# The first norm's sums as products, four modulation blocks as products, and rotary angles computed first

## The chip, the cores and the metric

The kernel is one program on one core of a Trainium2 chip. The metric is device time in microseconds (us). The kernel before takes 1474.31 us, the median of three runs (1472.94 to 1475.11).

## The reference, cut to what matters

A trunk of two layers with 512 tokens and 1024 features, in float32. Only the start of layer 0 matters here.

```python
cond = silu(c)                                    # c: (1, 1024)
mod = cond @ ada_w[l] + ada_b[l]                  # 6144 values: shift, scale, gate, twice
h = rms_norm(x, norm_mix[l]) * (1 + scale) + shift
proj = h @ w_in_even                              # MLA columns and RWKV-7 columns
y_a = mla_mix(proj[..., :MLA_COLS], positions)    # rotary angles: positions * inv_freq
y_b = rwkv7_mix(proj[..., MLA_COLS:])             # 8 heads of 64, a scan over tokens
```

Layer 0 sends the two mixers' outputs through one output projection, then comes a feed-forward block; layer 1 is another linear recurrence and a second feed-forward block.

## The kernel before, in words

The activations lie transposed: features on the 128 partitions, tokens along the free dimension, so `xT[0..7]` are eight tiles of 128x512. Each weight tile is split into a high part (the float32r cast of `split`, ScalarE, L192) and the remainder (VectorE, L193), and `mm3` (L212 to L214) multiplies high by high, low by high and high by low. I call each of these 128x512 products a **main product**.

The engines are TensorE (PE; PEld is its weight load), VectorE (DVE), ScalarE (ACT), GpSimd (POOL) and SyncE (SP), which issues all loads here. Each engine runs its own instructions in program order; the scheduler that builds the program sets this order by priorities and estimated times, so an instruction of a later part can stand between those of an earlier one.

The start runs so:

- `cond` is one row. ScalarE takes its Silu (L287), then two PE products with a row of ones (L431) spread it over 128 partitions, and two copies (L432) bring it back to SBUF.
- The first norm: ScalarE squares each `xT[k]` (`Stats.add`, L268), VectorE adds the eight squares up (L266, L259), PE sums them over partitions by four 128x1 products (L275), `rsqrt` is ten small VectorE operations (L228 to L243), and `token_bc` spreads the result by four products (L283).
- Modulation: `ada(l, j)` loads one 128x1024 block of `ada_w` in two halves, multiplies each by `cond` on VectorE with a running sum (L301), and ScalarE adds the bias (L308) and makes the gain (L312).
- Then for each k, `mod_tile` makes the high and low parts of h (L317, L320, L321), a weight tile is loaded and split, and 18 main products follow: 144 in all. The first one needs L320 of k = 0.

After that come the four head pairs p = 0 to 3 of RWKV. `rw_prep` is a chain over all engines: sums of squares (L510), `rsqrt`, a transpose (L250), a scan, `k2` (L533), a product (L540), and the scaled operands (L551 to L560). `a_mats` then makes the 32 small blocks by products (L573), which VectorE and ScalarE copy out (L576, L581). Main products of later projections fill PE between these. After pair 3 a triangular system is solved on VectorE (L617 to L647), and PE goes on with its result at L658. Projections and scores of MLA lie beside it.

The rotary angles (L808 to L825) are computed with features on partitions, in seventeen VectorE steps over 128x512 elements (a cast, a multiplication, and three range reductions with L815, L816 and L818 among them), then one Sin on ScalarE goes into `trig`.

## Time and profile before

| | |
|---|---|
| median of three runs | 1474.31 us |
| profiled execution, its own time | 1476.02 us |
| span of its profile (first to last instruction) | 1473.7 us |
| busy: PE, DVE, ACT, POOL | 1414.1, 851.9, 574.7, 21.7 us |
| granted TensorE clock, mean | 0.975 |

The span and the 2.3 us around it make the profiled execution's time. PE is busy for 96% of the span, so what matters is where PE has nothing to do and where it runs below its full clock. In the page's 40 slices of 36.8 us that is the first slice, where PE is busy for half the time, and slices 4 to 7 (110 to 258 us), where it is busy for seven to nine tenths and its granted clock is lower in places.

### The profile page before, as it was taken

What the parts mean: (1) busy time and instruction counts of PE and PEld (TensorE: products, weight loads), DVE (VectorE), ACT (ScalarE), POOL (GpSimd) and SP (SyncE); (2) the same over time, 40 slices, a digit from 0 to 9 for tenths busy, and PEclk for the clock granted to TensorE, in tenths of its full rate; (3) what the DMA queues carried; (4) which work ended last, traced back from release to release, by engine and by line L of the source; (5) the groups of instructions that cost most, each with busy time, mean ns of one, the idle gap of its engine ahead of it and who ended that gap; (6) DMA issues with size and microseconds to landing.
All of it is one profiled execution on the core that took longest, in us unless ns stands there. A gap on an engine that the chain in (4) does not pass through costs nothing.

```text
span 1473.7 us, 21313 instructions
## 1 busy us (share of the span) xinstructions
PE 1414.1 (96%) x8526; PEld 1126.2 (76%) x8526; DVE 851.9 (58%) x1683; ACT 574.7 (39%) x1018; POOL 21.7 (1%) x38
## 2 busy tenths in 40 slices
PE   5999978989999999999999999999999999999996
PEld 4776748867778878888888777777788888888885
DVE  6887795687787765333347566566574333333343
ACT  4665536455554342222235444444343222222220
POOL 2000000000000000000000000000000000000000
PEclk9998897989999999999999999999999999999998
DMA  8630221063548875322232221211123223322221
GB/s 279 212 102 36 72 101 59 9 215 115 190 151 276 266 241 182 118 97 92 70 109 74 101 73 59 73 69 62 54 77 129 86 70 99 118 99 97 64 84 58
DMA packets 57061, 167.06 MB, mean 113 GB/s; under 512 B 6337, under 2 KB 6913, under 8 KB 56962
## 3 DMA queue, kind: packets, MB, share of 16 engines
q1 hardware_dynamic: 56962, 165.70, 33.7%
q8 instruction: 67, 1.10, 0.3%
q14 instruction: 32, 0.26, 0.1%
HBM read 163.58 MB, written 2.10 MB: 112 GB/s over the span
## 4 chain that ended last, share of the span: by engine, by line
PE 85%; DVE 9%; ACT 2%; DMA 2%; issue 1%; SPq 0%; POOL 0%; DVEq 0%; ACTq 0%; POOLq 0%
PE t L212 24%; PE t L214 24%; PE t L213 23%; DVE t L301 2%; DMA t<-in_ada 1%; PE t L573 1%; DVE t L193 1%; PE t L250 1%; PE t L928 1%; PE t L908 1%; PE t L1063 1%; PE t L1076 1%; PE t L721 1%; PE t L727 1%; PE t L275 1%
## 5 line engine op out<-in xcount | busy, mean ns | idle before, releaser
L212 PE MATMUL t<-t,t 128*128 128x512 f32 x1632 | 652.6, 400 | 6.4 <-ACT t L320 4.8
L213 PE MATMUL t<-t,t 128*128 128x512 f32 x1632 | 650.9, 399 | 1.6 <-DVE t L193 1.5
L214 PE MATMUL t<-t,t 128*128 128x512 f32 x1632 | 648.1, 398 | 1.4 <-DVE t L193 1.3
L193 DVE TENSOR_TENSOR t<-t,t 128x1024 fp32r<-128x1024 f32 (+3 forms) x287 | 286.5, 1013 | 254.0 <-ACT t L192 251.4
L192 ACT CAST t<-t 128x1024 fp32r<-128x1024 f32 (+3 forms) x287 | 247.9, 879 | 341.0 <-PE t L214 175.0
L212 PEld LDWEIGHTS t<-t,t 128*128 128x128 f32 x1632 | 308.8, 189 | 76.5 <-ACT t L320 5.9
L213 PEld LDWEIGHTS t<-t,t 128*128 128x128 f32 x1632 | 308.5, 189 | 72.7 <-DVE t L193 4.2
L214 PEld LDWEIGHTS t<-t,t 128*128 128x128 f32 x1632 | 308.4, 189 | 71.1 <-DVE t L193 1.9
L301 DVE SCALAR_TENSOR_TENSOR t<-t,cond 128x512 f32<-128x512 f32 (+1 forms) x128 | 119.8, 952 | 20.9 <-DMA t<-in_ada 20.5
L390 DVE TENSOR_TENSOR t<-t,t 128x512 f32<-128x512 f32 x44 | 30.4, 690 | 89.6 <-PE t L214 89.6
L389 ACT ACTIVATE t<-t 128x512 f32<-128x512 f32 x42 | 25.0, 595 | 127.0 <-PE t L214 127.0
L330 DVE SCALAR_TENSOR_TENSOR t<-t,mod,t 128x512 f32<-128x512 f32 x40 | 29.8, 750 | 56.1 <-PE t L214 56.1
L306 ACT ACTIVATE mod<-t,c_prm 128x1 f32<-128x1 f32 x64 | 18.7, 295 | 93.6 <-DVE t L301 93.5
L908 PE MATMUL t<-t,t 128*128 128x128 f32 (+3 forms) x64 | 26.1, 514 | 8.1 <-DVE t L904 6.0
L268 ACT ACTIVATE t<-t 128x512 f32<-128x512 f32 x40 | 25.0, 629 | 18.3 <-DVE t L330 14.0
L320 ACT ACTIVATE t<-t,mod 128x512 fp32r<-128x512 f32 x32 | 22.4, 720 | 22.3 <-DVE t L317 22.3
L928 PEld LDWEIGHTS t<-t,t 128*128 128x128 f32 x160 | 23.3, 205 | 9.9 <-ACT t L926 7.2
L1083 DVE TENSOR_TENSOR t<-t,t 128x256 f32<-128x256 f32 x56 | 23.5, 419 | 10.4 <-PE t L1076 10.4
L250 PE MATMUL t<-cst,t 128*128 128x128 f32 x148 | 24.0, 287 | 3.4 <-DVE t L878 1.4
L928 PE MATMUL t<-t,t 128*128 128x64 f32 x160 | 25.5, 291 | 0.7 <-ACT t L926 0.7
L1063 PEld LDWEIGHTS t<-t,t 128*32 128x32 f32 x1280 | 13.9, 112 | 14.6 <-issue 9.9
L317 DVE SCALAR_TENSOR_TENSOR t<-t,gA,t 128x512 f32<-128x512 f32 x32 | 23.2, 741 | 2.9 <-PE t L283 2.9
(251 smaller groups left out, 1120.6 us busy)
## 6 DMA issues: line engine op xcount, KB each, us to landing
t<-in_ada SPq DMA_DIRECT2D x64, 512.0 KB, 4.3
t<-in_fu SPq DMA_DIRECT2D x44, 512.0 KB, 3.3
t<-in_fg SPq DMA_DIRECT2D x44, 512.0 KB, 3.3
t<-in_win SPq DMA_DIRECT2D x40, 512.0 KB, 3.2
t<-in_ada SPq DMA_DIRECT2D x64, 256.0 KB, 4.7
t<-in_fd SPq DMA_DIRECT2D x32, 384.0 KB, 3.1
t<-in_fd SPq DMA_DIRECT2D x32, 320.0 KB, 2.9
t<-in_xT SPq DMA_DIRECT2D x16, 256.0 KB, 3.9
```

The source lines that it names most:

```text
L192: S_.copy(hi[:, :n], raw[:, :n])
L193: V.tensor_tensor(out=lo[:, :n], in0=raw[:, :n], in1=hi[:, :n].bitcast(F32), op=ALU.subtract)
L212: TE.matmul(ps, a, xh, start=first and q == 0, stop=False)
L213: TE.matmul(ps, b, xh, start=False, stop=False)
L214: TE.matmul(ps, a, xl, start=False, stop=last and q == n - 1)
L250: TE.transpose(ps[:, blk(b)], src[:, blk(b)], ident)
L301: V.scalar_tensor_tensor(out=w, in0=w, scalar=1.0, in1=cond[:, n:n + m], op0=ALU.mult, op1=ALU.mult, accum_out=a[:, q:q + 1])
L330: V.scalar_tensor_tensor(out=xT[k], in0=ps, scalar=gate, in1=xT[k], op0=ALU.mult, op1=ALU.add)
L390: V.tensor_tensor(out=sg, in0=dense(PA, I[f"fu{l}"][j], hs), in1=sg, op=ALU.mult)
L908: TE.matmul(sps[:, :nk], mla["q"][:, blk(i)], kT[par][:, :nk], start=True, stop=True)
L928: TE.matmul(ops[:, i * 64:(i + 1) * 64], pT[:, blk(j)], vn[j][:, h * 64:(h + 1) * 64], start=j == 0, stop=j == i)
L1063: TE.matmul(lps[w:w + 32, c * 16:c * 16 + 16], kk[:, sl], half(q[:, sl], 1), start=True, stop=True, tile_position=(0, w))
```

## The change

1. `ada_pe` computes the modulation blocks j = 8, 0, 9, 1 (scale and shift of k = 0 and 1) on PE: the block is loaded with input features on partitions and multiplied by `condT`, `c` as eight columns, in eight 128x1 products each. Blocks 8 and 0 stand ahead of k = 0, 9 and 1 ahead of k = 1. The four blocks are loaded into `A_all`, whose memset moves behind the projection.
2. The squares of the first norm are no longer added by VectorE: each goes to PE at once, four 128x1 products for each k, 32 in all.
3. The angles are computed at the start, with tokens on partitions: 64 values on a partition, then 256. Sin stays where it was, on a broadcast view; four PE transposes and a copy make `trig`.
4. ScalarE issues four small loads (`cT`, the identity, positions, frequencies); `prm` is loaded between `xT[3]` and `xT[4]`.
5. `k2` of `rw_prep` is done by ScalarE. The sums of squares of the MLA latents take four products for each of five tiles (20) in the place of eight products and three VectorE adds.

```diff
     cond = cp.tile([P, D], F32, name="cond")
     nc.sync.dma_start(out=cond[0:1], in_=I["c"])
+    condT = cp.tile([P, KT], F32, name="condT")
+    nc.scalar.dma_start(out=condT, in_=I["cT"])
+    cst = cp.tile([P, CST.n], F32, name="cst")
+    nc.scalar.dma_start(out=cst[:, :P], in_=I["cst"][:, :P])
     xT = [X_() for _ in range(KT)]
-    for k in range(KT):
-        nc.sync.dma_start(out=xT[k], in_=I["xT"][k])
-    prm = load(cp, "prm", PRM.n)
...
     S_.activation(cond[0:1], cond[0:1], AF.Silu)
+    S_.activation(condT, condT, AF.Silu)
...
+    def ada_pe(l, j, ap, w, ps):
+
+        nc.sync.dma_start(out=w, in_=ap)
+        for k in range(KT):
+            TE.matmul(ps, w[:, blk(k)], condT[:, k:k + 1], start=k == 0, stop=k == KT - 1)
+        scales(l, j, ps, bias=pr("ada_b", 48 * l + j))
...
+        pos, freq = trig[:, :NB].bitcast(I32), w[:, 2 * n:2 * n + 16]
+        nc.scalar.dma_start(out=pos, in_=I["pos"])
+        nc.scalar.dma_start(out=freq, in_=I["freq"])
+        for k in range(KT):
+            nc.sync.dma_start(out=xT[k], in_=I["xT"][k])
+            if k == 3:
+                nc.sync.dma_start(out=prm, in_=I["prm"])
...
+            reduce(TWO_PI * 4096.0, [c * 4096.0 for c in (PI2_A, PI2_B, PI2_C)])
+            reduce(TWO_PI, (PI2_A, PI2_B, PI2_C))
...
-            G.memset(A_all, 0.0)
...
-                stats = Stats(D, M_)
+                ss, cols = PP(), PP()
                 for k in range(KT):
-                    stats.add(xT[k])
-                stats.close()
-                rb = token_bc(stats.end(PP), PP)
+                    sq = M_()
+                    S_.activation(sq, xT[k], AF.Square)
+                    for b in range(NB):
+                        TE.matmul(ss[:, b:b + 1], sq[:, blk(b)], ones, start=k == 0 and b == 0,
+                                  stop=k == KT - 1 and b == NB - 1)
+                first = lambda j, i: ada_pe(0, j, I["ada0p"][i], A_all[:, 1024 * i:1024 * i + 1024], cols[:, i:i + 1])
+                first(8, 0)
+                w = wload(I["win0a"][0], 768)
+                first(0, 1)
+                rb = token_bc(rsqrt(ss[:, :NB], NB, 1.0 / D, EPS), PP)
                 ps6 = [PA() for _ in range(6)]
                 for k in range(KT):
-                    ada(0, 8 + k, RP)
-                    ada(0, k, RP)
+                    if k == 1:
+                        first(9, 2)
+                        first(1, 3)
+                    elif k:
+                        ada(0, 8 + k, RP)
+                        ada(0, k, RP)
                     hs.append(mod_tile(0, 0, k, rb, M_, HR))
...
+            G.memset(A_all, 0.0)
...
-                V.tensor_scalar(out=k2, in0=a, scalar1=pr("k_a", p), scalar2=oka[:, p:p + 1],
-                                op0=ALU.mult, op1=ALU.add)
+                S_.activation(k2, a, AF.Identity, scale=pr("k_a", p), bias=oka[:, p:p + 1])
...
-        V.tensor_scalar(out=ang, in0=ang, scalar1=cs_("invf"), scalar2=None, op0=ALU.mult)
...
-        S_.activation(trig, ang, AF.Sin)
+        sin = X_()
+        S_.activation(sin.rearrange("p (b w s) -> p b w s", b=NB, w=2),
+                      trig[:, :256].rearrange("p (b s) -> p b s", b=NB).unsqueeze(2).to_broadcast([P, NB, 2, 64]), AF.Sin)
+        ps = PO()
+        transpose4(ps, sin)
+        S_.copy(trig, ps)
...
-            if j in (0, 2):
-                acc = sq
-            else:
-                V.tensor_tensor(out=acc, in0=acc, in1=sq, op=ALU.add)
...
+            for b in range(NB):
+                TE.matmul(sums[:, 4 * q + b:4 * q + b + 1], sq[:, blk(b)], means[:, q:q + 1],
+                          start=j == 0 and b == 0, stop=j == 4 and b == NB - 1)
```

The order of instructions moves in three places that matter below. The first is PE's start. Before, from its first row on (L431 spreads `cond`, L275 sums the squares, L283 spreads the norm, L212 is the first main product):

```order
L431 MATMUL t_133<-cond,trig 128x512
L431 MATMUL t_136<-cond,trig 128x512
L275 MATMUL t_187<-ones,t_164 128x1 x4
L283 MATMUL t_207<-cst,t_205 128x128 x4
L212 MATMUL t_212<-t_237,t_243 128x512
```

After, from the products of the eighth square on (L510; 28 like them stand ahead, behind the two that spread `cond`; L310 are the blocks 8 and 0, L279 is `token_bc`, L208 the first main product):

```order
L510 MATMUL t_190<-ones,t_234 128x1 x4
L310 MATMUL t_191<-condT,t_167 128x1 x8
L279 MATMUL t_282<-cst,t_280 128x128 x4
L310 MATMUL t_191<-condT,t_167 128x1 x8
L208 MATMUL t_287<-t_295,t_253 128x512
L209 MATMUL t_287<-t_295,t_254 128x512
```

Behind the two products that spread `cond`, 52 products now stand ahead of the first main product, where 8 stood. After the first 18 main products come 16 more of L310 (blocks 9 and 1).

The second place is PE at pair 2, behind L540 (L592 now), whose result VectorE needs for nothing that L573 (L625 now) reads. Before:

```order
L214 MATMUL t_2370<-t_567,t_2366 128x512
L212 MATMUL t_2407<-t_237,t_2403 128x512
L540 MATMUL t_1180<-t_906,cst 128x512
L573 MATMUL t_1199<-t_1184,t_1186 128x128 x2
L573 MATMUL t_1207<-t_1184,t_1186 128x128
L573 MATMUL t_1199<-t_1185,t_1187 128x128 x2
L573 MATMUL t_1207<-t_1184,t_1186 128x128
```

After, where 18 main products stand between L592 and the first L625; these are the last four of them and what follows:

```order
L208 MATMUL t_2414<-t_622,t_2410 128x512
L209 MATMUL t_2414<-t_622,t_2411 128x512
L210 MATMUL t_2414<-t_623,t_2410 128x512
L208 MATMUL t_2455<-t_295,t_2451 128x512
L625 MATMUL t_1256<-t_1241,t_1243 128x128 x2
L625 MATMUL t_1264<-t_1241,t_1243 128x128
L625 MATMUL t_1256<-t_1242,t_1244 128x128 x2
```

The pair's products L573 came right behind L540; now a row of main products lies between. Up to the first L573 of pair 3, PE has 420 main products in both orders.

The third place is VectorE at pair 2, just ahead of these products (L557 and L559 make what L573 reads, L818 is a step of the angles). Before:

```order
L541 TENSOR_TENSOR bv_125<-t_1180,t_1047 128x512
L553 TENSOR_TENSOR t_1185<-t_1129,t_1138 128x2x2
L560 TENSOR_TENSOR t_1186<-t_1058,t_1131 128x2x2x64
L557 SCALAR_TENSOR_TENSOR t_1129<-t_1129,t_1056 128x512
L818 SCALAR_TENSOR_TENSOR t_2343<-t_2342,t_2343 128x512
L559 TENSOR_TENSOR t_1186<-t_1129,t_1131 128x2x128
L559 TENSOR_TENSOR t_1187<-t_1129,t_1131 128x2x128
L560 TENSOR_TENSOR t_1187<-t_1058,t_1131 128x2x2x64
L818 SCALAR_TENSOR_TENSOR t_2343<-t_2342,t_2343 128x512
L456 SCALAR_TENSOR_TENSOR t_1262<-t_1237,c_prm,t_1262 128x511
```

After, the same rows of the pair (L609 and L611 are L557 and L559):

```order
L612 TENSOR_TENSOR t_1243<-t_1115,t_1188 128x2x2x64
L609 SCALAR_TENSOR_TENSOR t_1186<-t_1186,t_1113 128x512
L611 TENSOR_TENSOR t_1243<-t_1186,t_1188 128x2x128
L611 TENSOR_TENSOR t_1244<-t_1186,t_1188 128x2x128
L612 TENSOR_TENSOR t_1244<-t_1115,t_1188 128x2x2x64
L497 SCALAR_TENSOR_TENSOR t_1319<-t_1294,prm,t_1319 128x511
L628 COPY_PREDICATED t_167<-msk,t_1256 128x4x128
```

The steps of the angles are gone from between the pair's operations. Elsewhere on VectorE, in the solve from L617 to the last L647, the weight splits L193 fall from four to three, the adds L843 from two to none, the modulation steps L301 from four to two and the steps L904 from two to one; the adds are removed, and the others stand ahead of the solve or behind it.

## Rows read from the trace of the kernel before

**Rows 1.** Page, parts 1 and 4: busy time by engine; the chain that ended last.
```profile
PE 1414.1 (96%) x8526; PEld 1126.2 (76%) x8526; DVE 851.9 (58%) x1683; ACT 574.7 (39%) x1018; POOL 21.7 (1%) x38
...
PE 85%; DVE 9%; ACT 2%; DMA 2%; issue 1%; SPq 0%; POOL 0%; DVEq 0%; ACTq 0%; POOLq 0%
```

**Rows 2.** Timeline of the first 40 us: start, us, engine, line, operation, idle before it.
```profile
0.73 1.28 ACT L287 ACT_TABLE_LOAD   x1 [0.73 <-PEq L1208]
...
1.15 3.67 SPq L163 DMA_DIRECT2D t<-in_xT  x8
...
2.28 1.05 ACT L287 ACTIVATE cond<-cond 1x1024 f32<-1x1024 f32 x1 [0.27 <-DMA cond<-in_c]
...
3.38 3.78 PE L431 MATMUL t<-cond,trig 1*128 1x512 f32 x4 [3.38 <-ACT cond L287]
...
9.98 1.15 ACT L268 ACTIVATE t<-t 128x512 f32<-128x512 f32 x2
...
13.51 1.86 PE L275 MATMUL t<-ones,t 128*128 128x1 f32 x8 [6.34 <-DVE t L259]
...
15.41 0.16 DVE L228 TENSOR_SCALAR t<-t 128x4 f32<-128x4 f32 x1 [1.35 <-PE t L275]
...
19.38 0.15 DVE L243 TENSOR_TENSOR t<-t,t 128x4 f32<-128x4 f32 x1
...
19.59 2.07 PE L283 MATMUL t<-cst,t 128*128 128x128 f32 x8 [4.22 <-DVE t L243]
...
21.41 0.30 ACT L308 ACTIVATE t<-t,half_b 128x2 f32<-128x2 f32 x1 [0.41 <-DVE t L301]
...
22.49 0.72 ACT L320 ACTIVATE t<-t,mod 128x512 fp32r<-128x512 f32 x1
...
23.26 0.80 PE L212 MATMUL t<-t,t 128*128 128x512 f32 x1 [1.59 <-ACT t L320]
...
24.28 0.63 PE L212 MATMUL t<-t,t 128*128 128x512 f32 x1
...
24.71 0.63 PE L213 MATMUL t<-t,t 128*128 128x512 f32 x1
```

**Rows 3.** Windows: stretch, us, busy time of PE, PEld, DVE, ACT, POOL, granted clock, DMA.
```profile
40.00:50.00 10.00, 10.00 (x44) 8.00 (x44) 10.00 (x26) 5.83 (x17) 0.00 (x0) 1.00 0.95 323
...
135.47:155.00 19.53, 19.17 (x65) 15.54 (x66) 11.98 (x28) 8.83 (x15) 0.00 (x0) 0.50 0.16 54
...
175.00:222.00 47.00, 36.29 (x155) 25.54 (x155) 44.64 (x93) 17.97 (x36) 0.00 (x0) 0.93 0.26 90
...
420.50:423.40 2.90, 0.00 (x1) 0.00 (x0) 2.19 (x4) 1.52 (x4) 0.00 (x0) 1.00 0.79 305
...
424.66:428.08 3.42, 3.42 (x8) 2.75 (x9) 3.42 (x6) 2.41 (x5) 0.00 (x0) 0.50 0.00 0
```

**Rows 4.** Timeline of PE near 788 us: four 128x1 products between main products.
```profile
787.93 0.95 PE L275 MATMUL t<-ones,t 128*128 128x1 f32 x8
...
788.74 0.48 PE L212 MATMUL t<-t,t 128*128 128x512 f32 x1
```

**Rows 5.** Timeline of PE, 110 to 140 us: pair products before and in the slow stretch.
```profile
111.40 2.05 PE L573 MATMUL t<-t,t 64*128 64x128 f32 x16
...
135.47 3.78 PE L573 MATMUL t<-t,t 64*128 64x128 f32 x16 [2.84 <-DVE t L559]
```

**Rows 6.** The chain that ended last, 0 to 245 us: start, us, engine, line.
```profile
118.37 1.07 PE t L510 x8
...
150.71 1.50 PE t L510 x8
```

**Rows 7.** Groups of DVE by line, 175 to 220 us: xcount, busy, mean ns, idle before.
```profile
L193 DVE TENSOR_TENSOR t<-t,t 128x1024 fp32r<-128x1024 f32 x4 | 4.9, 1216 | 0.1
...
L301 DVE SCALAR_TENSOR_TENSOR t<-t,cond 128x1024 f32<-128x1024 f32 x4 | 4.8, 1212 | 0.0
...
L843 DVE TENSOR_TENSOR t<-t,t 128x512 f32<-128x512 f32 x2 | 1.4, 682 | 0.0
```

More of the change, by code (lines that the diff above doesn't have):

```diff
@@ L71 @@
 CST = Cols()
-for _n, _k in (("ident", 128), ("cent", 128), ("BB", 128), ("B2", 2), ("invf", 1), ("phase", 1)):
+for _n, _k in (("ident", 128), ("cent", 128), ("BB", 128), ("B2", 2)):
     CST.add(_n, _k)
@@ L95, in _const_arrays @@
     put(c, CST, "B2", np.stack([i < 64, i >= 64], 1))
-    f = np.concatenate([INV_FREQ, INV_FREQ, -INV_FREQ, INV_FREQ])
-    put(c, CST, "invf", np.concatenate([f, f])[:, None])
-    ph = np.concatenate([np.full(32, np.pi / 2), np.zeros(32)])
-    put(c, CST, "phase", np.concatenate([ph, ph])[:, None])
     s, t = i[:, None] % 64, i[None] % 64
@@ L160, in _body @@
     nc.sync.dma_start(out=cond[0:1], in_=I["c"])
+    condT = cp.tile([P, KT], F32, name="condT")
+    nc.scalar.dma_start(out=condT, in_=I["cT"])
+    cst = cp.tile([P, CST.n], F32, name="cst")
+    nc.scalar.dma_start(out=cst[:, :P], in_=I["cst"][:, :P])
     xT = [X_() for _ in range(KT)]
-    for k in range(KT):
-        nc.sync.dma_start(out=xT[k], in_=I["xT"][k])
-    prm = load(cp, "prm", PRM.n)
-    cst = cp.tile([P, CST.n], F32, name="cst")
-    nc.sync.dma_start(out=cst[:, :P], in_=I["cst"][:, :P])
+    prm = cp.tile([P, PRM.n], F32, name="prm")
     ones, means = cp.tile([P, 1], F32, name="ones"), cp.tile([P, 2], F32, name="means")
@@ L303, in ada, with scales @@
             n, q = n + m, q + 1
-        mod, i = mods[l][:, j:j + 1], 48 * l + j
+        i = 48 * l + j
         if q == 1:
-            S_.activation(mod, a[:, 0:1], AF.Identity, bias=pr("ada_b", i))
+            scales(l, j, a[:, 0:1], bias=pr("ada_b", i))
         else:
-            S_.activation(a, a, AF.Identity, bias=half_b[:, i:i + 1], accum_out=mod)
+            scales(l, j, a, bias=half_b[:, i:i + 1], accum_out=mods[l][:, j:j + 1])
+    def ada_pe(l, j, ap, w, ps):
[3 more added lines that the diff above has]
+        scales(l, j, ps, bias=pr("ada_b", 48 * l + j))
+    def scales(l, j, src, **kw):
+        mod = mods[l][:, j:j + 1]
+        S_.activation(mod if "accum_out" not in kw else src, src, AF.Identity, **kw)
         for s, name, o in ((0, "norm_mix", 8), (1, "norm_ffn", 32)):
@@ L424, in _body @@
         trig = lp.tile([P, T], F32, name="trig")
-        onesr = trig[0:1, :P]
+        n = NB * 16
+        w = M_()
+        pos, freq = trig[:, :NB].bitcast(I32), w[:, 2 * n:2 * n + 16]
[5 more added lines that the diff above has]
+                nc.sync.dma_start(out=prm, in_=I["prm"])
+                V.tensor_single_scalar(out=half_b, in_=pr("ada_b", 0, 96), scalar=0.5, op=ALU.mult)
+        onesr = M_()[0:1, :P]
         V.memset(onesr, 1.0)
@@ L432, in _body, with reduce @@
                 (V.tensor_copy if q else S_.copy)(cq, ps)
+            posf = t_(4)
+            V.tensor_copy(posf, pos)
+            ang, turns = w[:, :n], w[:, n:2 * n]
+            V.tensor_tensor(out=ang.rearrange("p (b f) -> p b f", b=NB), in0=posf.unsqueeze(2).to_broadcast([P, NB, 16]),
+                            in1=freq.unsqueeze(1).to_broadcast([P, NB, 16]), op=ALU.mult)
+            def reduce(turn, consts):
+                V.tensor_scalar(out=turns, in0=ang, scalar1=1.0 / turn, scalar2=MAGIC, op0=ALU.mult, op1=ALU.add)
+                V.tensor_scalar(out=turns, in0=turns, scalar1=-MAGIC, scalar2=None, op0=ALU.add)
+                for c in consts:
+                    V.scalar_tensor_tensor(out=ang, in0=turns, scalar=-c, in1=ang, op0=ALU.mult, op1=ALU.add)
+            reduce(TWO_PI * 4096.0, [c * 4096.0 for c in (PI2_A, PI2_B, PI2_C)])
+            reduce(TWO_PI, (PI2_A, PI2_B, PI2_C))
+            small = ang.rearrange("p (b f) -> p b f", b=NB)
+            ang, turns = trig[:, :4 * n], trig[:, 4 * n:]
+            big = ang.rearrange("p (b s f) -> p b s f", b=NB, s=4)
+            V.tensor_scalar(out=big[:, :, 0:2], in0=small.unsqueeze(2).to_broadcast([P, NB, 2, 16]),
+                            scalar1=float(np.float32(np.pi / 2)), scalar2=None, op0=ALU.add)
+            V.tensor_scalar(out=big[:, :, 2], in0=small, scalar1=-1.0, scalar2=None, op0=ALU.mult)
+            V.tensor_copy(big[:, :, 3], small)
+            reduce(TWO_PI, (TWO_PI,))
+            V.tensor_scalar(out=ang, in0=ang, scalar1=3.1415925, scalar2=-3.1415925, op0=ALU.min, op1=ALU.max)
         A_all = AB()
@@ L839, in _body @@
             S_.activation(sq, ps, AF.Square)
-            if j in (0, 2):
-                acc = sq
-            else:
-                V.tensor_tensor(out=acc, in0=acc, in1=sq, op=ALU.add)
-            if j in (1, 4):
-                q = j // 2 // 2
-                for b in range(NB):
-                    TE.matmul(sums[:, 4 * q + b:4 * q + b + 1], acc[:, blk(b)], means[:, q:q + 1],
-                              start=j == 1 and b == 0, stop=j == 4 and b == NB - 1)
+            q = 0 if j < 2 else 1
+            for b in range(NB):
+                TE.matmul(sums[:, 4 * q + b:4 * q + b + 1], sq[:, blk(b)], means[:, q:q + 1],
+                          start=j == 0 and b == 0, stop=j == 4 and b == NB - 1)
         ckv, cq = lat[:2], lat[2:]
```

23 lines of the change are left out of this document (5 added, 18 removed).

## The prediction

> **What bounds the kernel now.** I read the page first: PE is busy for 1414.1 of 1473.7 us, and 85% of the chain that ended last is PE's [rows 1]. So a change pays where PE waits or runs slowly, and costs wherever it gives PE work that no wait covers. Then I read the timeline of the first 40 us. The last square ends at 9.98 + 1.15 = 11.13, the sum on VectorE lets PE begin its four 128x1 products at 13.51, `rsqrt` runs from 15.41 to 19.53 with steps of `ada` between its operations, PE spreads the norm from 19.59, and the first main product starts at 23.26 [rows 2]. From there PE is full: 40 to 50 us has no idle time, at 10.00/44 = 0.23 us a main product [rows 3]. At the start the step is 24.71 - 24.28 = 0.43 us [rows 2], nearly twice that. So PE begins at the lower of its two clock levels (1.2 GHz).
>
> Third, the windows after 110 us. Ahead of pair 2's products PE waits 2.84 us for VectorE's L559 [rows 5]. Right behind this wait the granted clock is 0.50 (1.2 GHz) from 135.47 to 155.00, though PE is busy for 19.17 of 19.53 us [rows 3]; sixteen records of L573 take 3.78 us where the pair before took 2.05 [rows 5]. From one pair's sums of squares to the next it is 150.71 - 118.37 = 32.3 us [rows 6]. Last, the solve: from 175 to 222 us VectorE is busy for 44.64 of 47 us and PE for 36.29 [rows 3], so VectorE's load sets when PE can go on, and PE has 10.7 us to spare.
>
> **The head.** All of PE's products ahead of the first main product are in one row now, so I add them up.
> - ScalarE issues four loads before its table load. SP needed 3.67/8 = 0.46 us an issue [rows 2]; I take 0.43 for smaller ones, so 1.7 us (bounds 0 and 1.8). The table load (1.28) then ends at 0.73 + 1.7 + 1.28 = 3.7, the Silu of `condT` at 4.0 (an activation of few columns took 0.30), and the Silu of `cond` (1.05) at 5.05 [rows 2]. It ended at 3.33 before.
> - PE spreads `cond` in 3.78 us [rows 2], to 8.85.
> - 32 products of squares: four took 1.86 us at the start, 0.465 each [rows 2], and 0.81 us at the high level near 788 us (787.93 to 788.74), 0.2025 each [rows 4]. At the low level 32 take 14.9 us, to 23.7. The squares are there long before (11.13 plus some tenths, as `prm` is loaded between them).
> - Eight products of block 8: 3.7 us, to 27.4. `rsqrt` lies under them: ten operations of 0.16 us [rows 2] and no `ada` steps between.
> - `token_bc` 2.07 us [rows 2], to 29.5; block 0, 3.7 us, to 33.2; then ScalarE's bias step (0.30) and the high part (0.72) [rows 2], to about 34.3.
>
> The first main product starts near 34.4 instead of 23.26: **+11.1 us**. VectorE's removed adds and `ada` steps, and the angle steps at the start, lie beside this and count nothing; without that cover some twenty small angle operations would cost 3 to 4 us (an estimate from the 0.16 us of a small one).
>
> Which level PE has in this row decides, and the trace shows no long run of 128x1 products. The nearest stretch is 135.47 to 155.00: PE 98% busy, the weight load 80%, and 0.50 throughout [rows 3]. I take the lower level; the upper one is a rival. On this the Trainium skill speaks (TensorE: Matmul & The Clock Gate, "Why this matters for your kernels"): it says that matmuls kept going without a break bring the full clock, and by that the row from 5 us on would run fast and the sum would be the first rival's. The stretch above is busy and stays slow, so the rule alone doesn't carry it.
>
> **The products of blocks 9 and 1.** They stand between the first 18 main products and the next, so nothing covers them. 16 x 0.2025 = 3.2 us at the high level (7.4 at the low). The second block waits for ScalarE's bias step of the first (some 0.4), and the next main product for ScalarE's bias step and the high part, 0.30 + 0.72 [rows 2], 1.1 with the hand-overs. That makes 4.7 us without main products. After 2.90 us of idle PE near 420 us, the clock was at 0.50 for 3.42 us [rows 3]; as half of that is lost, 1.7. Together **+6.4 us** (3.2 if the clock holds and the waits vanish, 9 if these products run slowly too).
>
> **Pair 2.** The angle steps are gone from between the pair's operations, and 18 main products (4.2 us) stand ahead of L573, so the wait of 2.84 goes, and with it what came behind. Of the 19.2 busy us at 0.50, two rows of L573 took 7.5 and take 4.1 at the high level; the other 11.7 take half. That is 3.4 + 5.8 = 9.2. Both orders have 420 main products up to pair 3's L573, so nothing else moves the count. **-12.0 us** (bounds: -2.8 if the clock falls here anyway, -14 if pair 3, which begins in the slow stretch, gains more). `k2` on ScalarE takes 0.5 us off VectorE in each pair, where PE has main products to do: nothing, at most -2.
>
> **The solve.** Fewer foreign operations lie in VectorE's chain: one L193 (1.2), two L301 (2.4) and two L843 (1.4) [rows 7], and one L904, a half-height operation that I take as an L843 (0.7). These are 5.7 by duration; VectorE has 2.4 us idle there, and the chain's own dependencies will leave some of the gain unused. I take **-3.9 us** (bounds 0 and -5.7). PE's twelve more 128x1 products for the latents (2.4) and four transposes (0.5) fall into the 10.7 us to spare: nothing, 2.9 without that cover. The memset moved on POOL has the time of the whole projection until `a_mats`.
>
> **Sum.** 11.1 + 6.4 - 12.0 - 3.9 = +1.6 us. The profiled execution took 1476.0 (span 1473.7 and 2.3 around it), 1.7 above the median of 1474.3, so I put the sum on the median: **1475.9 us, no change**. Two tenths of a per cent, 2.9 us, is what a measurement of this kernel can tell from nothing.
>
> **The rivals.**
> - *PE runs the head at its upper level.* For it speaks that PE's row has no gap from 5 us on; against it the slow busy stretch [rows 3]. Then the 32 products end at 8.85 + 6.5 = 15.3, block 8 at 17.0, the spreading (about half of 2.07) at 18.3 and block 0 at 19.9; the first main product comes at 21.0, 2.3 earlier. The twelve main products that ran at 0.43 run at 0.23, -2.4, and the blocks 9 and 1 cost 4.7. So 0 - 12.0 - 3.9 = -15.9: **1458 us**.
> - *VectorE isn't what the solve waits for* (slower). If its chain is set by dependencies, the foreign operations only fill gaps, and taking them out gives nothing. For it: the ten small operations of `rsqrt` leave gaps. Against it: 44.64 of 47 us busy. Then +1.6 + 3.9 = +5.5: **1480 us**. It decides once less than 2.6 of the 3.9 us come.
> - *The small things go well.* Issues on ScalarE cost next to nothing (-1.7) and the clock holds over the sixteen products (-1.7): **1472.5 us**.
> - *The angles leave, but pair 2 stays slow*, as another operation fills VectorE: +9.2, **1485 us**. Against it: the order has 4.2 us of main products there. I give it little.
>
> **How the numbers follow.** My forecast 0.46 (its own range 1472 to 1479.5; 0.34 within 0.2%, 0.12 above), the upper level 0.16 (all faster), the solve 0.20 (all slower), the small things 0.14 (half faster, half within), pair 2 0.04 (slower). So faster 0.23, same 0.41, slower 0.36. The range reaches from 1463, which takes in a head at the upper level for part of its way, to 1481; it leaves out the full first rival and pair 2, 0.20.
>
> **What would show it.** Right: the products of squares 0.46 us apart, the first main product near 34 us, a stretch at 0.50 soon after blocks 9 and 1, no wait ahead of pair 2's products and 1.00 behind them, and L617 to the last L647 some 4 us shorter. Wrong: steps of 0.20 in the squares (the first rival), a solve as long as before (the second), or a clock at 0.50 in pair 2 or 3. What I can't bound well is whether the clock falls once more or once less in later gaps; one such stretch was worth 1.7 us near 425 us.

## The result, and the profile of the changed kernel

The changed kernel took 1489.24 us (median of four executions, 1487.5 to 1491.0) where the kernel before took 1474.71: a ratio of 1.0082, interval 1.0054 to 1.0110. In a second comparison (twelve executions, below) it was 1484.76, ratio 1.0050, interval 1.0033 to 1.0068. It is slower, by 14.5 us in the first comparison and by 7.0 (1484.76 against 1477.72) in the second; I had forecast 1475.9 and no change, and the range ended at 1481.

The page of the changed kernel, parts 1 and 4:

```profile
PE 1438.8 (97%) x8674; PEld 1150.2 (77%) x8674; DVE 837.0 (56%) x1655; ACT 578.0 (39%) x1020; POOL 21.8 (1%) x38
...
PE 83%; DVE 7%; DMA 5%; ACT 3%; issue 1%; ACTq 0%; DVEq 0%; SPq 0%
```

PE's span grew by 14.1 us, its busy time by 24.7 [rows 1]; it waits less and works more. The timeline of PE at the start shows where (start, us, engine, line, operation, idle before it; two records make one of the 128x1 products):

```profile
5.10 3.78 PE L448 MATMUL t<-cond,t 1*128 1x512 f32 x4 [5.10 <-ACT cond L283]
8.81 13.81 PE L510 MATMUL t<-ones,t 128*128 128x1 f32 x64
22.48 3.55 PE L310 MATMUL t<-condT,t 128*128 128x1 f32 x16
25.90 2.05 PE L279 MATMUL t<-cst,t 128*128 128x128 f32 x8
27.74 3.41 PE L310 MATMUL t<-condT,t 128*128 128x1 f32 x16
32.26 0.80 PE L208 MATMUL t<-t,t 128*128 128x512 f32 x1 [1.10 <-ACT t L327]
...
39.17 1.84 PE L310 MATMUL t<-condT,t 128*128 128x1 f32 x16
41.36 3.52 PE L310 MATMUL t<-condT,t 128*128 128x1 f32 x16 [0.35 <-ACT mod L315]
45.99 0.80 PE L208 MATMUL t<-t,t 128*128 128x512 f32 x1 [1.11 <-ACT t L327]
```

The 32 products of squares (L510) take 22.48 - 8.81 = 13.67 us, 0.43 each: the lower level, as forecast. The first main product starts at 32.26, 9.0 behind [rows 2]. The main products start in steps of 0.43, and of 0.23 from 38.2 on. The first of blocks 9 and 1 (L310 at 39.17) runs at 0.23 a product, the second (41.36) at 0.44: the level fell between them, and main products come again at 45.99, in steps of 0.43. The windows (as in [rows 3]) say the same, and that pair 2's slow stretch is gone:

```profile
38.00:41.00 3.00, 3.00 (x22) 2.69 (x20) 0.00 (x0) 0.00 (x0) 0.00 (x0) 1.00 0.66 236
41.00:46.00 5.00, 3.54 (x18) 3.45 (x17) 2.00 (x6) 1.70 (x5) 1.06 (x1) 0.54 0.00 0
46.00:51.00 5.00, 5.00 (x12) 3.94 (x13) 5.00 (x11) 2.44 (x7) 5.00 (x1) 0.50 0.20 59
...
151.91:171.44 19.53, 18.83 (x100) 14.34 (x99) 13.18 (x28) 14.03 (x24) 0.00 (x0) 1.00 0.08 27
```

The granted clock is 1.00 from 38 to 41 us, 0.54 and 0.50 from 41 to 51 (twelve main products in 5.00 us), and 1.00 in the 19.53 us from pair 2's products on, where the kernel before had 0.50 in a stretch of the same length [rows 3].

To see which step cost what, I took the same events from PE's timeline of both traces. Of the kernel before: the first pair's sums of squares, pair 3's products, the first product of the inverses, and the main product that follows the first 1320, near the end of the first feed-forward part (below: the 1320th); pair 2's products are in [rows 5].

```profile
67.16 1.05 PE L510 MATMUL t<-cst,t 128*128 128x2 f32 x8 [0.19 <-ACT t L507]
...
167.72 2.05 PE L573 MATMUL t<-t,t 64*128 64x128 f32 x16
...
221.91 1.74 PE L658 MATMUL t<-t,t 32*32 32x32 f32 x32 [0.21 <-issue]
...
547.12 0.39 PE L212 MATMUL t<-t,t 128*128 128x512 f32 x1
```

Of the changed kernel, with pair 2's products second:

```profile
85.85 1.05 PE L563 MATMUL t<-cst,t 128*128 128x2 f32 x8 [0.19 <-ACT t L560]
...
151.91 2.05 PE L625 MATMUL t<-t,t 64*128 64x128 f32 x16
...
176.01 2.05 PE L625 MATMUL t<-t,t 64*128 64x128 f32 x16
...
228.37 1.74 PE L710 MATMUL t<-t,t 32*32 32x32 f32 x32 [1.02 <-issue]
...
556.34 0.39 PE L208 MATMUL t<-t,t 128*128 128x512 f32 x1
```

| up to | before | changed | behind | this step, forecast | measured |
|---|---|---|---|---|---|
| first main product (head) | 23.26 | 32.26 | +9.0 | +11.1 | +9.0 |
| first pair's sums (blocks 9, 1) | 67.16 | 85.85 | +18.7 | +6.4 | +9.7 |
| pair 3's products (pair 2) | 167.72 | 176.01 | +8.3 | -12.0 | -10.4 |
| first inverse (solve) | 221.91 | 228.37 | +6.5 | -3.9 | -1.8 |
| 1320th main product | 547.12 | 556.34 | +9.2 | 0 | +2.8 |
| end of the span | 1473.7 | 1487.8 | +14.1 | 0 | +4.8 |

With a second trace of each kernel (both below) the six steps are +10.1, +10.4, -9.3, -1.9, +2.5 and +3.3. Both traces of the changed kernel are of executions that took longer than its median of 1484.76 (1489.59 and 1491.01 us).

The last step is one place. VectorE and PE of the changed kernel at 551 to 566 us:

```profile
557.41 1.23 DVE L297 SCALAR_TENSOR_TENSOR t<-t,cond 128x1024 f32<-128x1024 f32 x1 [3.75 <-DMA t<-in_ada]
...
562.17 0.80 PE L208 MATMUL t<-t,t 128*128 128x512 f32 x1 [4.32 <-ACT t L188]
...
563.99 0.80 PE L210 MATMUL t<-t,t 128*128 128x512 f32 x1 [0.59 <-DVE t L189]
```

and of the kernel before at the same point of the program:

```profile
544.69 1.22 DVE L301 SCALAR_TENSOR_TENSOR t<-t,cond 128x1024 f32<-128x1024 f32 x1 [2.73 <-DMA t<-in_ada]
...
549.45 0.50 PE L212 MATMUL t<-t,t 128*128 128x512 f32 x1 [0.81 <-ACT t L192]
...
551.45 0.50 PE L214 MATMUL t<-t,t 128*128 128x512 f32 x1 [1.27 <-DVE t L193]
```

VectorE multiplies layer 1's modulation blocks there between its other work. It waits for a block's load (`in_ada`), 3.75 us where it was 2.73; the split of a weight (L189, before L193) stands behind that in its row, and PE waits 4.32 + 0.59 where it was 0.81 + 1.27, after which six of the changed kernel's main products have steps of 0.43 (1.2 us more than at 0.23).

### The profile page after: what moved, and what is told of

Same layout as the page of the kernel before. It is cut to its first block, busy times and chain, and to the rows that moved or that the text cites. A ratio compares the mean times of both kernels' runs of the same rounds, so it can differ in the third digit from the quotient of the medians.

```text
span 1487.8 us, 21583 instructions
## 1 busy us (share of the span) xinstructions
PE 1438.8 (97%) x8674; PEld 1150.2 (77%) x8674; DVE 837.0 (56%) x1655; ACT 578.0 (39%) x1020; POOL 21.8 (1%) x38
## 4 chain that ended last, share of the span: by engine, by line
PE 83%; DVE 7%; DMA 5%; ACT 3%; issue 1%; ACTq 0%; DVEq 0%; SPq 0%
PE t L208 22%; PE t L210 22%; PE t L209 22%; DMA t<-in_ada 4%; DVE t L297 2%; PE t L246 1%; PE t L963 1%; PE t L943 1%; DVE t L189 1%; PE t L1098 1%; PE t L510 1%; PE t L625 1%; PE t L310 1%; ACT t L188 1%; PE t L1111 1%
## 5 line engine op out<-in xcount | busy, mean ns | idle before, releaser
L208 PE MATMUL t<-t,t 128*128 128x512 f32 x1632 | 654.3, 401 | 10.6 <-ACT t L327 5.4
L189 DVE TENSOR_TENSOR t<-t,t 128x1024 fp32r<-128x1024 f32 (+3 forms) x287 | 286.7, 1014 | 255.4 <-ACT t L188 252.9
L208 PEld LDWEIGHTS t<-t,t 128*128 128x128 f32 x1632 | 309.3, 190 | 81.2 <-ACT t L188 6.7
L297 DVE SCALAR_TENSOR_TENSOR t<-t,cond 128x1024 f32<-128x1024 f32 (+1 forms) x120 | 114.6, 971 | 22.4 <-DMA t<-in_ada 21.9
L396 ACT ACTIVATE t<-t 128x512 f32<-128x512 f32 x42 | 25.0, 595 | 127.3 <-PE t L210 127.3
L315 ACT ACTIVATE mod<-t,prm 128x1 f32<-128x1 f32 x68 | 19.7, 292 | 115.5 <-DVE t L297 86.7
L327 ACT ACTIVATE t<-t,mod 128x512 fp32r<-128x512 f32 x32 | 22.4, 721 | 19.8 <-DVE t L324 19.8
L1118 DVE TENSOR_TENSOR t<-t,t 128x256 f32<-128x256 f32 x56 | 23.5, 420 | 10.5 <-PE t L1111 10.5
L328 DVE SCALAR_TENSOR_TENSOR t<-t,mod,t 128x512 fp32r<-128x512 f32 x32 | 23.7, 747 | 4.9 <-ACT t L327 4.8
L264 ACT ACTIVATE t<-t 128x512 f32<-128x512 f32 x32 | 20.0, 629 | 16.1 <-DVE t L337 14.0
```

The lines of the kernel that those rows point to most:

```text
L189: V.tensor_tensor(out=lo[:, :n], in0=raw[:, :n], in1=hi[:, :n].bitcast(F32), op=ALU.subtract)
L208: TE.matmul(ps, a, xh, start=first and q == 0, stop=False)
L297: V.scalar_tensor_tensor(out=w, in0=w, scalar=1.0, in1=cond[:, n:n + m], op0=ALU.mult, op1=ALU.mult, accum_out=a[:, q:q + 1])
```

## The experiments

Each ratio is to executions of the kernel before taken beside that run; their medians lie between 1476.4 and 1477.7 us.

**Blocks 9 and 1 back on VectorE.**
```diff
-                    if k == 1:
-                        first(9, 2)
-                        first(1, 3)
-                    elif k:
+                    if k:
                         ada(0, 8 + k, RP)
                         ada(0, k, RP)
```


> The changed kernel, with blocks 9 and 1 taken back to VectorE; all else stays. Theory 'local' (each part costs at its own place, and what it costs is carried unchanged to the end): the first main product stays at 32.3 us, the stretch from 39.2 to 46.0 with sixteen 128x1 products falls away, the granted clock stays at 1.00 behind the first 18 main products, and the first pair's sums of squares come 9.7 us earlier (18.7 us behind before becomes 9.0). Time 1489.2 - 9.7 = 1479.5 us. Rival 'absorbed' (VectorE, which gets four operations of 0.6 us for each block back, is then late for the norm's tiles, and a wait on it takes the place of the products): less than half comes, 1484 us or more.

1478.85 us, ratio to the kernel before 1.0004 (0.9987 to 1.0021). The first main product is at 32.26 as before the edit, and the granted clock stays up (windows):

```profile
41.00:46.00 5.00, 5.00 (x23) 4.03 (x22) 4.91 (x13) 2.68 (x8) 0.00 (x0) 1.00 0.93 307
```

The first pair's sums come at 77.02, 9.86 behind the kernel before instead of 18.69: 8.8 of the 9.7 us of this step came back, and the time against the kernel before fell from 1.0050 or 1.0082 to 1.0004. The theory of a local loss holds; PE is busy for all of the 5.00 us, so no wait took the products' place.

**Squares back on VectorE.**
```diff
-                        for b in range(NB):
-                            TE.matmul(ss[:, b:b + 1], sq[:, blk(b)], ones, ...)
+                stats = Stats(D, M_)
+                for k in range(KT):
+                    stats.add(xT[k])
+                stats.close()
...
-                rb = token_bc(rsqrt(ss[:, :NB], NB, 1.0 / D, EPS), PP)
+                rb = token_bc(stats.end(PP), PP)
```


> The changed kernel, with the squares summed on VectorE and four products at the end, as before the change; all four blocks stay products. Theory 'local': the 32 products at 0.43 us are what holds the first main product; it comes at about 21.5 us (squares done near 11.5, four products, ten small operations, spreading, bias step and high part), 10.7 earlier; time about 1478.5 us. Rival 'the blocks hold it too': the sixteen products of blocks 8 and 0 take 7 us at the lower level and stand ahead of the four products in PE's row; the first main product comes at 25 us or later and the time is 1482 us or more.

1479.90 us, 1.0017 (0.9996 to 1.0037). PE's row:

```profile
13.30 3.57 PE L310 MATMUL t<-condT,t 128*128 128x1 f32 x16 [4.43 <-DMA t<-in_ada0p]
16.74 1.84 PE L271 MATMUL t<-ones,t 128*128 128x1 f32 x8
18.45 3.55 PE L310 MATMUL t<-condT,t 128*128 128x1 f32 x16
...
23.70 3.41 PE L310 MATMUL t<-condT,t 128*128 128x1 f32 x16
28.50 0.79 PE L208 MATMUL t<-t,t 128*128 128x512 f32 x1 [1.38 <-ACT t L327]
```

and VectorE's last addition of the squares:

```profile
14.62 0.69 DVE L255 TENSOR_TENSOR t<-t,t 128x512 f32<-128x512 f32 x1
```

The first main product comes at 28.50, not 21.5: only 3.8 of the 9.0 us came back. The rival was right, though not alone: block 8 waits for its load until 13.30, the sums (L271) stand behind it in the row, and three blocks (8, 0 and 9: sixteen records each) stand ahead of the first main product, 10.5 us by their rows. But VectorE has the squares summed only at 14.62 + 0.69 = 15.31, where I had taken 11.5 and the kernel before has 13.46, as the angle steps stand between its additions; of the sums' start at 16.74 block 8 can account for 1.4 us at most. Behind it only block 1 is left, at the upper level; PE is 5.2 behind the kernel before at the first main product and 9.0 at the sixtieth (9.0 and 18.6 in the changed kernel).

**The angles alone computed first**, in the kernel before.
```diff
+            posf = t_(4)
+            V.tensor_copy(posf, pos)
+            ang, turns = w[:, :n], w[:, n:2 * n]
...
-        S_.activation(trig, ang, AF.Sin)
+        ps = PO()
+        transpose4(ps, sin)
+        S_.copy(trig, ps)
```


> The kernel before, with the rotary angles alone computed first (tokens on partitions, with their four transposes); squares, blocks, latents and k2 as before. Theory 'local': the wait of 2.8 us ahead of pair 2's products goes and the clock there stays at 1.00, worth the 10.0 us that the changed kernel gained between 130 and 176 us; 1474.7 - 10 = 1464.7 us, one or two less if VectorE's freer row helps the solve. Rival 'given back': the layer-1 modulation loads that run beside the first feed-forward part are what comes due at 557 us whatever is gained ahead of them, and their wait of 4.7 us appears here too: 1469.5 us. Second rival: the angle steps delay VectorE's sums in the head, 1 to 3 us of the gain lost there.

1472.82 us, 0.9962 (0.9944 to 0.9981): faster, by about half of what I expected. From the first pair's sums to pair 3's products 9.2 us are gained (to the first inverse 10.4), but the first main product is at 28.63, 5.4 late. The head's timeline:

```profile
0.73 6.92 POOL L476 MEMSET t<- 128x8192 f32 x1 [0.29 <-POOLq L1226]
...
2.43 5.25 DVE L440 CAST t<-trig 128x4 f32<-128x4 int32 x1 [1.36 <-DMA trig<-in_pos]
...
12.27 3.87 DVE L266 TENSOR_TENSOR t<-t,t 128x512 f32<-128x512 f32 x5
...
28.63 0.80 PE L212 MATMUL t<-t,t 128*128 128x512 f32 x1 [1.60 <-ACT t L320]
```

In the changed kernel, where the memset stands behind the head (at 44.94), the same cast is

```profile
5.02 0.17 DVE L453 CAST t<-trig 128x4 f32<-128x4 int32 x1 [3.95 <-DMA trig<-in_pos]
```

The cast takes 5.25 us and ends with POOL's memset (0.73 to 7.65), the angle steps follow to 12.3, and the first of the sums (L266), which starts at 5.13 in the kernel before, starts at 12.27. The second rival of the expectation was right, at more than its 1 to 3 us; the first one, a longer wait at 557 us, did not come (80 main products from the 1320th on took 21.5 us, 21.1 in the kernel before).

**The angles in their new form, behind the head.** The same code and its two loads, placed behind the line that builds `pre`.
```diff
                 pre = {j: shifted(j, ps6[j], ...) for j in (5, 4, 0, 2, 3, 1)}
+            nc.sync.dma_start(out=pos, in_=I["pos"])
+            nc.sync.dma_start(out=freq, in_=I["freq"])
+            posf = t_(4)
...
```

> The kernel before, with the rotary angles in their new form (tokens on partitions, four transposes) computed right behind the projections of the first norm instead of ahead of its sums; nothing else changed. Theory 'VectorE's row in the head': in the run with the angles ahead of the sums the first main product came at 28.6 us instead of 23.3, because the sums stood behind the angle steps on VectorE; behind the projections these steps lie under main products, so the head is that of the kernel before (23.3 us), and the gain between pair 2 and pair 3 stays (9 to 10 us). That is 5 us less than the run with the angles ahead, some 1466 us, 10 below the kernel before. Rival 'VectorE is full there too': the steps push the pairs' operations back by their 4.4 us, a wait of some microseconds appears ahead of pair 0's or pair 1's products, and half of the gain goes: 1470 us or more.

1473.24 us, 0.9968 (0.9949 to 0.9987). The head is that of the kernel before (first main product at 22.89), pair 3's products come 6.8 us early and the first inverse 5.7; the rival's side of the expectation is nearer by its time, but not by its mechanism: PE waits ahead of no pair's products there. The order on PE moved instead: 444 main products stand ahead of pair 3's products where the kernel before has 420, and up to the first inverse both have 504. So the 6.8 us compare unlike amounts of work, and the 5.7 at the inverse compare like ones. From pair 3's products to the inverse it took 55.2 us (54.2 in the kernel before), though 24 main products fewer were left for it.

**The angles in their new form, at their old place**, in the kernel before.
```diff
-        V.tensor_copy(ang, pos)
-        V.tensor_scalar(out=ang, in0=ang, scalar1=cs_("invf"), scalar2=None, op0=ALU.mult)
+        nc.sync.dma_start(out=freq, in_=I["freq"])
+        posf = t_(4)
+        V.tensor_copy(posf, pos)
...
```

> The kernel before, with the angles in their new form at their old place in the program, between pair 2's operations; nothing else changed. The steps there take 4.4 us of VectorE instead of 9.2. Theory 'fewer VectorE steps are enough': 4.8 us less ahead of pair 2's products is more than the wait of 2.8, so the wait and the slow stretch behind it go and the time is within 2 us of that with the angles behind the head, about 1467 us. Rival 'the place counts': angle steps still stand in pair 2's chain, a wait of one microsecond or more stays and the granted clock still falls to 0.50: 1473 us or more.

1467.15 us, 0.9934 (0.9909 to 0.9959): the lowest time of this study, below both. Pair 2's products come with no wait listed before them, and the window of 20 us around and behind them has the clock at 1.00:

```profile
131.79 2.05 PE L573 MATMUL t<-t,t 64*128 64x128 f32 x16
...
131.00:151.00 20.00, 19.27 (x103) 14.89 (x102) 15.97 (x37) 15.45 (x26) 0.00 (x0) 1.00 0.17 54
```

Pair 3's products come 11.2 us early (8.2 against the second trace of the kernel before). In the kernel before the angle steps are seventeen VectorE operations on 128x512, 9.1 us between 122 and 153 us; with tokens on partitions they are on 128x64 to 128x256 and take 4.3, all but the cast between 121 and 139 us, still among pair 2's operations. So the early place is not what pair 2 needed. The smaller steps were enough, though not by VectorE alone: the order on PE moved with them, and ten main products stand between L540 and pair 2's products where the kernel before has none. No run separates the two.

**Eighteen wide products near the start of the squares.**
```diff
+                wide = M_(F32R)
+                S_.activation(wide, cond[:, :T], AF.Copy)
+                dps = PA()
+                for q in range(18):
+                    TE.matmul(dps, wide[:, :P], wide, start=q == 0, stop=q == 17)
```


> The changed kernel, with eighteen 128x512 products of no use (of a copy of cond, into a PSUM tile that nobody reads) in PE's row near the start of the 32 products of squares; one activation of ScalarE makes their operand. Theory 'narrow products don't keep the high level': the eighteen take 7 to 8 us at 0.43, the level rises during them or not, and within a few microseconds of 128x1 products the steps are 0.43 again: the first main product comes 6 us or more later than 32.3, time 1494 us or more. Rival 'once up, PE stays up while its row has no gap': behind the eighteen the squares run at 0.20 to 0.23, the head's 128x1 products take half, the first main product comes at 27 to 31 us, and the first main products run at 0.23: 1484 us or less.

1484.31 us, 1.0044 (1.0026 to 1.0062), with 6.6 us more work on PE than the changed kernel. PE's timeline, and the window behind it:

```profile
9.02 3.58 PE L515 MATMUL t<-ones,t 128*128 128x1 f32 x16
12.46 6.78 PE L510 MATMUL t<-t 128*128 128x512 f32 x18
19.07 5.41 PE L515 MATMUL t<-ones,t 128*128 128x1 f32 x48
24.35 3.45 PE L310 MATMUL t<-condT,t 128*128 128x1 f32 x16
...
41.73 0.80 PE L208 MATMUL t<-t,t 128*128 128x512 f32 x1 [0.96 <-ACT t L327]
...
24.30:41.70 17.40, 15.77 (x74) 15.52 (x73) 2.38 (x11) 2.44 (x8) 0.86 (x1) 0.50 0.01 4
```

Eight products of squares at 0.43, the wide ones (18 in 6.61), then 24 products of squares in 5.28 us: 0.22 each, the upper level. From 24.35 on, with no gap in the row at that point, a product of a block takes 0.43 again, and the window reads 0.50. Each theory is half right: the level rose during the wide products and was kept for 24 products of squares, and in the row of 128x1 products it fell again. All four blocks stand ahead of the first main product here, which comes at 41.73; at the sixtieth PE is 1.2 us ahead of the changed kernel, for all the added work.

**A third buffer for the modulation blocks** of the feed-forward part, in the changed kernel.
```diff
-            M_, A_, AD = pools(st, 8, (22, T, F32R), (2, 1024))
+            M_, A_, AD = pools(st, 8, (22, T, F32R), (3, 1024))
```


> The changed kernel, with three buffers in place of two for the modulation blocks that VectorE works through beside the feed-forward part. Theory 'the landings set it' (with two buffers a load can start only when VectorE has used up the block two ahead, so a landing of 5 or 6 us holds up VectorE, and behind it the split of the weights): the wait of 4.3 us near 558 us and the slow stretch behind it go, 1489.2 - 5 = 1484 us. Rival 'VectorE or the transfer rate sets it': the wait stays within 1 us of 4.3, 1488 to 1489 us.

1486.41 us, 1.0052 (1.0034 to 1.0069). From 555 to 590 us PE waits for nothing any more, but near 430 us, where the changed kernel's only long wait is one of 2.9, there are two:

```profile
434.31 2.05 PE L279 MATMUL t<-cst,t 128*128 128x128 f32 x8 [2.83 <-DVE t L239]
440.29 0.79 PE L208 MATMUL t<-t,t 128*128 128x512 f32 x1 [3.93 <-ACT t L327]
```

Four blocks of VectorE now come between the ten small operations of the second norm, which take from 428.14 to 434.15 us (one block and 425.47 to 428.43 in the changed kernel). The sixtieth main product is as far behind the kernel before as in the changed kernel (18.5), the 900th 16.8 instead of 9.2. The 80 main products from the 1320th on take 18.5 us here, so the wait near 557 us is gone, as the theory of buffers and landings says; the gain was given away ahead of it.

**The changed kernel once more**, and **the kernel before once more.**

> The changed kernel once more, unaltered, for a second trace and twelve more times. Theory 'the loss at 557 us belongs to the program': PE again waits 4 us or more for the split of a down-projection weight there, and the median is 1488 us or more. Rival 'it belonged to that execution' (single landings of the modulation loads of 5 to 6.4 us, where 4.4 is usual): the wait is that of the kernel before (about 2 us in all), and the median lies nearer 1485 us.

1484.76 us (1480.1 to 1491.0). The new trace:

```profile
558.02 1.23 DVE L297 SCALAR_TENSOR_TENSOR t<-t,cond 128x1024 f32<-128x1024 f32 x1 [4.59 <-DMA t<-in_ada]
...
PE t L208 <- ACT t L188: 5.0, 1, 5.0
```

Up to the 1320th main product the two traces of the changed kernel agree within 0.1 us (556.34, 556.27); the 80 products behind it take 25.8 and 27.7 us. So the long wait came again, as the theory says, but the median came out on the rival's side, 1484.76.

> The kernel before, unaltered, for a second trace. In its first trace 80 main products around the last down-projections of the first feed-forward part (from 547.1 us) took 21.1 us, where 80 at 0.23 take 18.5; in the two traces of the changed kernel the same 80 took 25.9 and 27.7. Theory 'the landings of one execution set this': up to the 1320th main product the two traces of the kernel before agree within 0.3 us, and behind it they differ, by anything up to 7 us. Rival 'it belongs to the program': 21.1 again, within 0.5.

Its longest wait there:

```profile
PE t L212 <- ACT t L192: 1.9, 1, 1.9
```

The 80 products take 24.3 us where they took 21.1. Up to there this execution is 2.7 us ahead of the first one (1.8 of it by the thirtieth main product), so "within 0.3" was wrong. In the run with the narrow angles they took 19.8. So this place differs by 2 to 3 us between two executions of one program and by 8 over the traces of this study with two buffers (19.8 to 27.7), against the 4.8 of my table. That the twelve times above go from 1480 to 1491 though the first 556 us repeat within 0.1 points the same way. The changed kernel has the two longest of them all (the others reach 24.9), but both executions are among its longer ones; whether the change also shifts the mean of this wait, four traces don't tell.

**k2 and the latents' sums**, added to the run with the narrow angles at their old place; then the latents' alone.
```diff
-                V.tensor_scalar(out=k2, in0=a, scalar1=pr("k_a", p), scalar2=oka[:, p:p + 1], ...)
+                S_.activation(k2, a, AF.Identity, scale=pr("k_a", p), bias=oka[:, p:p + 1])
...
-                V.tensor_tensor(out=acc, in0=acc, in1=sq, op=ALU.add)
+            q = 0 if j < 2 else 1
```


> The run with the narrow angles at their old place, and on top of it the two parts of the change that belong to the solve: k2 on ScalarE, and the latents' squares summed by products alone. Step of the prediction under test: VectorE's load sets the solve, so what leaves VectorE there shortens it. In the run with the narrow angles alone it takes 55.3 us from pair 3's products (156.5) to the first inverse (211.8). Theory 'VectorE sets it': four operations of 0.52 us and three of 0.68 us leave VectorE's row, 52 to 53 us, time some 2.5 us below that run (1464 to 1465 us where it had 1467). Rival 'dependencies set it': no gain, and twelve more products of 128x1 stand in PE's row, up to 5 us at 0.43 each where nothing covers them: 55 to 58 us, time the same or up to 3 us above.

> The run with the narrow angles at their old place, and on top of it the latents' squares summed by products alone (k2 stays on VectorE). It splits the run with both: theory 'VectorE sets the solve': about half of that run's gain, 1 to 1.5 us; rival 'dependencies': none, and what the twelve further products cost shows here alone.

1468.48 us (0.9948, 0.9929 to 0.9966) and 1469.38 (0.9962, 0.9947 to 0.9977). From pair 3's products to the first inverse it took 52.2 and 53.8 us instead of 55.3, as the theory says. But over all the traces this stretch does not follow VectorE's busy time in it (windows):

| run | stretch, us | VectorE busy, us |
|---|---|---|
| kernel before | 54.19 | 49.28 |
| changed kernel | 52.36 | 44.59 |
| angles alone first | 53.03 | 49.88 |
| blocks 9 and 1 back | 55.73 | 47.35 |
| narrow angles, old place | 55.27 | 49.56 |
| with the latents' part | 53.84 | 44.45 |
| with k2 and the latents' part | 52.23 | 44.43 |

The most VectorE work goes with the third shortest stretch, and two equal loads with 53.84 and 52.23. What leaves VectorE shortened the stretch in these two runs; that VectorE's load sets it is not shown. At the 900th main product the first of them is only 0.6 us ahead of the run without these parts, and the second 1.2 behind it: the gain was given back behind the solve, and neither time is below that of the run without them.

**Blocks 8 and 0 under the sums**, in the same base.
```diff
+                first(8, 0)
+                first(0, 1)
                 rb = token_bc(stats.end(PP), PP)
```


> The run with the narrow angles at their old place, with blocks 8 and 0 as products as in the change, but with the squares summed on VectorE as before, and blocks 9 and 1 on VectorE. PE waits there from 8.9 us to 13.5 and from 15.4 to 19.4. Theory 'under cover a product of 128x1 costs nothing': the sixteen products (7 us at 0.43) lie in these waits, the ten small operations of the norm run without modulation steps between them and end some 2 us earlier, and the first main product comes at 21 us instead of 23.1; time 2 us below that run, 1465 us. Rival 'the row is in order': products that wait for their block's load stand ahead of the sums or of the spreading, and the first main product comes at 23.1 or later; time the same or above.

1473.19 us, 0.9970 (0.9955 to 0.9986), some 5 us above its base by the two ratios. PE's head:

```profile
11.63 3.57 PE L317 MATMUL t<-condT,t 128*128 128x1 f32 x16 [4.22 <-DMA t<-in_ada0p]
...
16.77 3.55 PE L317 MATMUL t<-condT,t 128*128 128x1 f32 x16
20.18 2.06 PE L285 MATMUL t<-cst,t 128*128 128x128 f32 x8
23.98 0.80 PE L214 MATMUL t<-t,t 128*128 128x512 f32 x1 [1.75 <-ACT t L334]
```

Block 8 waits for its load to 11.63, the sums stand behind it, block 0 ahead of the spreading (L285), and the first main product comes at 23.98, 0.9 later than in the base. At the sixtieth main product it is 1.7 behind the base, at the first pair's sums 3.0, at the first inverse 3.4 and at the 900th main product 7.2; what is lost between I did not trace. The rival held.

## Why the prediction was wrong

**The head** was right in its mechanism: PE's one row of 128x1 products, at the lower level, holds the first main product. ScalarE's issues cost what I took (PE begins at 5.10 for 3.38 [rows 2]); the whole came 2.1 us earlier than the sum. Most of that is the price of a product: I took 0.465, a short row's length through four, and the steps are 0.43, which over 48 products makes 1.8. The first rival falls: no product of squares ran at 0.20. By the Trainium skill (TensorE: Matmul & The Clock Gate, "Why this matters for your kernels") matmuls without a break should have had the full clock. This trace does not agree: PE's row has no wait listed from 5.10 to 31 us and the steps say half, and in the run with the wide products it lost the level within such a row. "VectorE's angle steps at the start lie beside this and count nothing" holds only because the squares had left VectorE: with the sums there the steps and a 5.25 us cast cost 5.4, and without the long cast (squares back) the sums still end at 15.3.

**Blocks 9 and 1**: of the four terms of the sum the one that was mis-sized most, +9.7 for 6.4. I took the products at the upper level with the clock falling behind them. The level fell already between them: the second block took 3.52 us, the stall 45.99 - 39.17 = 6.8 instead of 4.7, and up to the sixtieth main product the slow steps cost 2.7 more instead of 1.7. Undoing these two blocks returned 8.8 us. My upper bound of 9 was itself too low, as it left out the slow main products for the case of slow blocks (7.4 + 1.5 + 1.7 = 10.6).

**Pair 2**: right in sign, and in what it frees: no wait, 1.00 behind, L625 in 2.05. It was 10.4 instead of 12.0. That this needs the early place, which the prediction took without a test, is wrong: the smaller operations do it at the old place, together with the order on PE that came with them, and without a cost in the head.

**The solve**: right in sign, -1.8 instead of -3.9. VectorE is busy there for 4.7 us less, and the stretch is only 1.8 shorter. By the prediction's own mark (less than 2.6 of the 3.9) this decides for the second rival, VectorE isn't what the solve waits for; but a gain of 1.8 us is not nothing, and in the two runs with less on VectorE the stretch is 1.5 and 3.1 shorter. So neither side holds as it was put, and what sets the solve the traces don't show. The third rival (the clock holds) and the fourth (pair 2 stays slow) didn't come.

**What I set at nothing**, everything behind the solve, is the step that failed by most: +7.6 us in the first pair of traces, +5.8 in the second, for 0. Between the first inverse and the 1320th product the changed kernel loses 2.8 us (2.5 in the second pair). All of it lies within the first 600 main products, for which it takes 134.2 and 134.4 us from the inverse on, the kernel before 131.4 and 131.6. The order of the operations differs there, and no run isolates a cause: the latents' part alone makes this stretch 1.3 longer than in its base, but the run with the squares back, which has that part too, takes 129.7. So this stays open. And the wait at the end of the first feed-forward part was on none of my lists: 2.1 us of PE's time in the trace that I had, which I took for fixed, and which changes from one execution to the next by more than the effect that I forecast. Every term but the head missed on the same side. Without the last row of the table the change costs 9.2 us where I had 1.6 (11.8 in the second pair of traces); it is blocks 9 and 1 (+3.3), the solve (+2.1), pair 2 (+1.6) and the open 2.8 that make the difference, less the 2.1 of the head. The median of the second comparison, 7.0 us behind, lies nearer to the forecast than either pair of traces (14.1 and 15.1).

## What to carry to other kernels

A price for a product with one moving column holds only for the place where it was read: four between main products took 0.20 us each [rows 4], a row of them at the start took 0.43, and the main products behind paid for it too. When VectorE is what is late, first make its operations smaller: changing the layout alone gave 9.3 us up to the 1320th main product against the first trace of the kernel before and 6.7 against the second, and each part that moved work to PE's row in the head (blocks 9 and 1, the squares, blocks 8 and 0 on the better base) took more than it gave where it was tested. Take two traces of the kernel before, and see which waits differ between them, ahead of forecasting a change of a few microseconds.

## What the runs showed that I had not expected

A VectorE cast of 128x4 took 5.25 us next to a POOL memset of 6.92 us and ended 0.03 us behind it; with the memset moved away (changed kernel) it took 0.17, and at its old place at 55 us (narrow angles), long behind the memset, 0.16. The kernel before has tensor-tensor additions next to the same memset (L266, 0.69 us, the same as elsewhere). The Trainium skill (SBUF — State Buffer, "SBUF: two separate sides") says that VectorE and GpSimd share a pair of ports, which an operation takes whole for its duration, and that only some kinds of VectorE operation need it. Both durations agree with that; that the ports are the cause no run here shows.

The granted clock in the windows of the changed kernel reads 1.00 from the start of the span, though the steps are 0.43 until 38 us: at the start the distance between products tells the level, not that column.
